# Two weight pieces multiplied side by side at the head of the dense layer and of the recurrent block, and the first two attention pairs' probabilities formed during the projections

## The chip, the cores and the metric

The kernel runs on one core of a Trainium2 chip. The metric is the device time of one execution in microseconds, from the first to the last instruction with what lies around it. The kernel before took 1434.54 us (median of three runs, 1433.47 to 1436.35). The profile is of one further execution of 1437.88 us, of which 1435.7 us are the span of its instructions.

## What is computed

Two layers over 256 tokens of width 1024 in float32. What matters for the change, cut from the reference:

```python
# layer 0
proj = h @ w_in                                   # q, k, v of 16 heads of 64, forget logits
p = softmax(q k^T / 8 + mask (+ F_t - F_s))       # causal; heads 8..15 with a forget bias
o = concat(p @ v) @ w_out
x = x + gate * rms_norm(o)                        # and the next sub-layer's norm and modulation
x = x + gate * rms_norm((silu(h @ w_gate) * (h @ w_up)) @ w_down)     # dense layer, d_ff 2816
# layer 1
proj = h @ w_in                                   # gate branch and u, 1280 each
conv = causal width-4 convolution of u
r, i = sigmoid(conv @ w_a + b_a), sigmoid(conv @ w_x + b_x)           # block diagonal, 10 blocks of 128
hs = linear recurrence; y = gelu(gate branch) * hs; y @ w_out
x = x + gate * rms_norm(...)
x = x + gate * rms_norm(top-2-of-8 expert SwiGLU)                     # d_expert 3584
```

The shifts, scales and gates of all norms come from `silu(c) @ w_ada`.

## The kernel before, in words

All products are made on TensorE (PE) in float32r as three matmuls, high part times high part, high part times low part of the activations, low part of the weights times high part (`mm3`, L404 to L407; a weight's two parts are `whi`, `wlo`, the activations' `hThi`, `hTlo`). One **piece** is 128 output columns of a weight with its 1024 rows: eight blocks of 128 rows, so 24 matmuls of 256 tokens, all into one PSUM bank (`wstat`, L409 to L413).

**The weights** come as one stream of 1 MB pages of two pieces each (class `Stream`). SyncE's queue loads them into six buffers (`raw`). Each piece is split into its two parts: ScalarE (ACT) rounds it to `whi` (L386), VectorE (DVE) subtracts to get `wlo` (L389). Between them the stream holds pieces of `w_ada`, which DVE multiplies and sums with `silu(c)` (L212, 1.2 us each, "ada" below); the tables `ADA_QK`, `ADA_SCORE` and `ADA_OUT` say how many ada pieces are taken at each step. `ws.done` frees a piece and lets later ones be loaded, split or reduced. Each engine runs its instructions in the order in which they were written; engines wait for each other only by semaphores.

**PSUM** has eight banks: four of the tag `B`, handed out in turn by `wbank()`, two of `t`, and `y0` and `y1`. A bank is given again only when the readers of its last use are done. The output projection, the dense layer's down product and the recurrent block's output product are summed in `y0`, `y1` and the two `t` (`y_banks`).

**Attention.** A loop of 16 steps makes the pieces q0, k0, q1, k1 to q7, k7 on PE, each copied out by ACT (L580 or L582); for the first eight DVE and GpSimd (POOL) apply the rotation (`rope`). At step 9 the forget logits are made on PE, and from step 9 on `forget()` spreads their sigmoid, logarithm and running sum, and some small vectors for layer 1, over DVE and ACT: an exponential (L543, L544), a logarithm (L546, L547), each with a load of ACT's function table. Then a second loop goes over p = 0 to 9, where p is a pair of heads: `scores(p)` (eight or sixteen matmuls on PE, then mask and row maximum on DVE, L613 to L617), `exps(p)` (ACT, L626), a reciprocal (DVE, L683) and `norms` (POOL, L634: four diagonal matrices `dg`), and two steps later `turn(p)` (PE, L641 to L643: transposes the probabilities and divides by their sums at once; ACT copies them to `pt`, L644), `heads_out(p)` (PE, L652; ACT copies to `o`, L655), and one step later `out_proj(p)` (PE, L661). So in pass p stand, in this order: scores(p), turn(p-2), exps(p), ada pieces, reciprocal and norms(p), out_proj(p-3), heads_out(p-2), ada pieces.

**Between sub-layers** `finish` applies the norm, PE transposes the result into the four `B` banks (L381), and `make_hT` (L394 to L402) turns it block by block into `hThi` and `hTlo`: ACT scales and shifts (L399), DVE rounds (L388) and subtracts (L389).

**Dense layer.** Six groups of four gate pieces (`fg`), four up pieces (`fu`) and four down pieces (`fd`); gate and up of one piece share a bank, the gate in columns 0 to 255. **Recurrent block.** Pieces `lu` 0 to 9 (the branch u), then `lg` 0 to 9. After each `lu` ACT and DVE run the convolution (L775, L778), ACT and DVE split its result (`ch`, `cl`), and two steps later PE makes the two gates of that block (`gates_mm`, L405 to L407 on `ch`, `cl`), which ACT turns into `rg` and `ig` (L799, L801) and DVE multiplies in (L802). Then come exponential, root and recurrence on ACT and DVE, and the output product `lo`. The experts follow, with most of the bytes.

Of the kernel before, what the change touches and what calls it, by code (L numbers as in the profile page):

```python
# [1 line left out]

# [6 lines left out]
F32 = mybir.dt.float32  # L9
# [121 lines left out]
def trunk_kernel(ctx, tc, xin, cbc, sm_d, at_d, wd, wm, out, stage=9):  # L131
# [282 lines left out]

    def y_banks():
        return [[bank("y0"), bank("y1")], [bank("t", 2), bank("t", 2)]]
# [151 lines left out]

    ADA_QK = [0, 0, 1, 1, 1, 0, 1, 1, 1, 2, 2, 1, 1, 1, 1, 1]
    ADA_SCORE = [2, 0, 1, 1, 2, 2, 3, 1, 3, 1]  # L570
    ADA_OUT = [0, 2, 1, 1, 1, 2, 0, 2, 0, 1]
    pend, fox = None, forget()
    for i in range(16):
        w = ws.next()
        kind, j = w[2]
        b = wbank()
        wstat(b[:, :S], w, hi, lo)
        if j < 4:
            qk32[kind, j] = poolH.tile([P, S], F32, name="qk32", tag="v32", bufs=4)
            A.activation(qk32[kind, j], b[:, :S], AF.Copy)  # L580
        else:
            A.activation(qk[kind, j], b[:, :S], AF.Copy)  # L582
        if i > 8:
            next(fox, None)
        ws.done(ada=ADA_QK[i])
        if pend:
            rope(*pend)
        pend = (kind, j) if j < 4 else None
    pb.close()

    pb = ExitStack()
    poolB = pb.enter_context(tc.tile_pool(name="poolB", bufs=1))
    mask = C("mask")
    pt4 = const.tile([P, 4, 384], F32, name="pt4", tag="hThi", bufs=1)

    def scores(p):
# [5 lines left out]
        sb = [wbank() for _ in range(2)]  # L602
# [42 lines left out]

    def heads_out(p):
        b = wbank()
        for kt in range(2):
            n = 256 - kt * P
            for hh in range(2):  # L650
                c = p * P + hh * 64
                T.matmul(b[hh * 64:hh * 64 + 64, :n], v32[:, kt, c:c + 64],  # L652
                         pt4[:, 2 * (p % 2) + hh, kt * 256:kt * 256 + n], start=kt == 0, stop=kt == 1)
        o = poolB.tile([P, S], F32, name="o", bufs=3)
        A.activation(o, b[:, :S], AF.Copy)  # L655
        return o
# [11 lines left out]
    probs, outs = {}, {}  # L668
    for p in range(10):
# [4 lines left out]
        if p == 7:  # L674
            ws.cap = 3
        if p < 8:
            res, mx = scores(p)
        if 0 <= p - 2 < 8:
# [27 lines left out]
    ws.done(1, ada=1)  # L706
    Y = y_banks()
    for c in range(6):
        n = 4 if c < 5 else 2
        bs = [wbank() for _ in range(n)]  # L710
        acts = []
        for j in range(n):
            w = ws.next("fg")
# [130 lines left out]
    for n in range(2 * N_RNN):  # L844
# [3 lines left out]
        if n < N_RNN:  # L848
            w = ws.next("lu")
            b = wbank()  # L850
            wstat(b[:, :S], w, hi, lo)
# [831 lines left out]
```

## Time and profile before

| | |
|---|---|
| median of three runs | 1434.54 us (1433.47 to 1436.35) |
| profiled execution | 1437.88 us, its span 1435.7 us |
| PE busy | 1380.0 us, 96% of the span |
| DVE busy | 892.1 us, 62% |
| ACT busy | 693.1 us, 48% |
| POOL busy | 44.5 us, 3% |
| bytes read | 474.32 MB, 331 GB/s over the span |
| mean granted TensorE clock | 0.991 of full speed |

A matmul's end in the profile is modelled, and a matmul that waits for an operand after its start was counted can look busy. So on PE the starts of the matmuls are read, and the distance between them, rather than the busy share. In order of time the span holds: attention with its projections to 165 us, the dense layer from 178 to 370 us, the recurrent block from 378 to 485 us, and the experts from there on.

### The profile page before, as it was taken

How to read it: one execution, taken by the hardware profiler on the slowest of the kernel's cores; microseconds unless marked ns; L12 is line 12 of the kernel's file. 1: busy time of each engine (PE TensorE's matmuls, PEld its weight loads, DVE VectorE, ACT ScalarE, POOL GpSimd, SP SyncE). 2: the span in 40 equal slices, each digit the busy share in tenths (PEclk: the TensorE clock that was granted, in tenths of full speed). 3: DMA queues.
4: the chain of work that ended last, by engine and by line, in shares of the span. 5: the costliest groups of instructions: out<-in, count | busy, mean ns of one | idle time of the engine just before them, and what ended most of it. 6: DMA issues, size and time to landing. Idle time of an engine off the chain costs nothing.

```text
span 1435.7 us, 21519 instructions
## 1 busy us (share of the span) xinstructions
PE 1380.0 (96%) x8223; PEld 1008.6 (70%) x8223; DVE 892.1 (62%) x1269; ACT 693.1 (48%) x1022; POOL 44.5 (3%) x62
## 2 busy tenths in 40 slices
PE   5989999999898899999999999999999999999997
PEld 2786589999797678877777767766566566665652
DVE  5787498874798789888666766755333343333321
ACT  2444454443685687976565656743222232321311
POOL 0106200000000000000000000000000000000000
PEclk9999999999999999999999999999999999999999
DMA  9976578886164988699999999999999999998991
GB/s 390 380 269 232 204 284 345 341 314 240 59 219 152 359 319 312 218 364 364 372 398 408 409 390 420 388 370 408 414 398 414 389 365 406 404 410 328 388 374 64
DMA packets 76989, 476.84 MB, mean 332 GB/s; under 512 B 8528, under 2 KB 8528, under 8 KB 28880
## 3 DMA queue, kind: packets, MB, share of 16 engines
q1 hardware_dynamic: 76880, 475.40, 84.8%
q8 instruction: 66, 1.08, 0.3%
q14 instruction: 43, 0.35, 0.1%
HBM read 474.32 MB, written 1.05 MB: 331 GB/s over the span
## 4 chain that ended last, share of the span: by engine, by line
PE 84%; DVE 7%; ACT 4%; DMA 2%; issue 2%; POOL 0%; SPq 0%; ACTq 0%; POOLq 0%; DVEq 0%
PE B L1064 18%; PE B L405 12%; PE B L406 12%; PE B L407 11%; PE y L1064 7%; PE y L407 3%; PE y L406 3%; PE y L405 3%; DVE wlo L389 2%; DMA raw<-in_wm_dram 2%; PE t L1155 1%; PE t L1337 1%; PE y L492 1%; DVE raw L212 1%; PE y L661 1%
## 5 line engine op out<-in xcount | busy, mean ns | idle before, releaser
L389 DVE TENSOR_TENSOR wlo<-raw,whi 128x1024 fp32r<-128x1024 f32 x451 | 541.2, 1221 | 231.5 <-ACT whi L386 196.2
L386 ACT ACTIVATE whi<-raw 128x1024 fp32r<-128x1024 f32 x448 | 465.0, 1057 | 261.4 <-PE B L407 183.9
L1064 PE MATMUL B<-raw,xTc 128*64 128x256 f32 x1792 | 205.3, 382 | 0.0
L405 PE MATMUL B<-hThi,whi 128*128 128x256 f32 x640 | 181.6, 284 | 2.2 <-ACT ge L831 1.7
L406 PE MATMUL B<-hTlo,whi 128*128 128x256 f32 x640 | 180.6, 282 | 0.8
L405 PE MATMUL B<-whi,xTh 128*128 128x512 f32 x448 | 181.3, 405 | 0.0
L407 PE MATMUL B<-hThi,wlo 128*128 128x256 f32 x640 | 178.6, 279 | 0.0
L406 PE MATMUL B<-wlo,xTh 128*128 128x512 f32 x448 | 176.9, 395 | 1.3 <-DVE srt L1384 0.7
L407 PE MATMUL B<-whi,xTl 128*128 128x512 f32 x448 | 176.6, 394 | 0.0
L1064 PEld LDWEIGHTS B<-raw,xTc 128*64 128x64 f32 x1792 | 124.3, 137 | 74.4 <-issue 16.5
L406 PEld LDWEIGHTS B<-hTlo,whi 128*128 128x128 f32 x640 | 120.0, 188 | 4.6 <-DVE hTlo L389 3.6
L405 PEld LDWEIGHTS B<-hThi,whi 128*128 128x128 f32 x640 | 120.2, 188 | 3.8 <-ACT ge L831 1.9
L407 PEld LDWEIGHTS B<-hThi,wlo 128*128 128x128 f32 x640 | 120.0, 187 | 0.0
L212 DVE CUSTOM_DVE_ANT_0 raw<-raw,cond 128x1024 f32<-128x1024 f32 x96 | 113.9, 1217 | 0.0
L405 PEld LDWEIGHTS B<-whi,xTh 128*128 128x128 f32 x448 | 84.1, 188 | 30.4 <-issue 13.2
L1064 PE MATMUL y<-raw,hTc 128*64 128x512 f32 x448 | 101.9, 596 | 0.0
L406 PEld LDWEIGHTS B<-wlo,xTh 128*128 128x128 f32 x448 | 84.2, 188 | 20.7 <-DVE wlo L389 3.6
L407 PEld LDWEIGHTS B<-whi,xTl 128*128 128x128 f32 x448 | 84.1, 188 | 19.5
L1143 DVE TENSOR_TENSOR sg<-sg,B 128x256 f32<-128x256 f32 x35 | 14.6, 418 | 95.6 <-ACT sg L1142 95.6
L1064 PEld LDWEIGHTS y<-raw,hTc 128*64 128x64 f32 x448 | 30.6, 137 | 54.4 <-issue 52.1
L405 PE MATMUL y<-whi,hTh 128*128 128x512 f32 x168 | 67.4, 401 | 0.4 <-ACT hTh L1163 0.4
L407 PE MATMUL y<-whi,hTl 128*128 128x512 f32 x168 | 66.5, 396 | 0.8 <-DVE hTl L1164 0.8
(314 smaller groups left out, 1605.0 us busy)
## 6 DMA issues: line engine op xcount, KB each, us to landing
raw<-in_wm_dram SPq DMA_DIRECT2D x261, 1024.0 KB, 8.8
raw<-in_wd_dram SPq DMA_DIRECT2D x114, 1024.0 KB, 6.4
raw<-in_wm_dram SPq DMA_DIRECT2D x150, 512.0 KB, 8.6
x<-in_x_dram SPq DMA_DIRECT2D x1, 1024.0 KB, 5.2
out_dram<-res SPq DMA_DIRECT2D x4, 256.0 KB, 2.7
sm<-in_sm_dram SPq DMA_DIRECT2D x1, 548.5 KB, 6.8
cond<-in_c_dram SPq DMA_DIRECT2D x1, 512.0 KB, 6.0
at<-in_at_dram SPq DMA_DIRECT2D x1, 320.0 KB, 9.3
```

The source lines that it names most:

```text
L212: V.tensor_tensor_reduce(src, src, cond, 1.0, 0.0, op0=ALU.mult, op1=ALU.add, accum_out=modc[:, col:col + 1])
L386: A.activation(hi, v32, AF.Copy)
L389: V.tensor_tensor(lo, v32, hi.bitcast(F32), op=ALU.subtract)
L405: T.matmul(o, lh, rh, start=start, stop=False)
L406: T.matmul(o, lh, rl, start=False, stop=False)
L407: T.matmul(o, ll, rh, start=False, stop=stop)
L492: T.matmul(vb[h][tt], whole[k][:, t], w[3][:, c], start=k == 0, stop=k == 7)
L661: T.matmul(Y[tt][h], o_of(o)(tt), w[3][:, h * 512:h * 512 + 512], start=p == 0, stop=end)
L1064: T.matmul(o[64 * t:64 * t + 64], xs, w[:, t * n:t * n + n], start=start, stop=stop)
L1143: V.tensor_tensor(g[t], g[t], b[:, 256:], op=ALU.mult)
L1155: T.transpose(b[:, j * P:(j + 1) * P], a[t][:, j * P:(j + 1) * P], ident)
L1337: T.matmul(b, u.pt[t][r, tt * P:(tt + 1) * P], yr[r, j], start=j == 0, stop=j == 1)
```

## The change

Three things are done, all in `trunk_kernel`:

- **Probabilities beside projections.** `scores`, `exps`, `norms` and `turn` are defined before the projection loop. A generator `first_probs(p)` makes scores(p), exps(p) and norms(p) of pairs 0 and 1 in three steps each; from step 10 of the projection loop on one step is taken after each piece. These two scores use the `t` banks. The second loop then starts at p = 2, where turn(0) stands ahead of scores(2). The ada pieces of the first two passes (two and two) are given to pass 2: three behind its exponentials instead of one, three at its end instead of one.
- **Dense layer.** The first two `fg` pieces are multiplied together (`wstat_pair`): for each block of 128 rows the three matmuls of the first piece and then the three of the second, into `y0` and `y1`; the other two of that group use `B`.
- **Recurrent block.** The same for `lu` 0 and `lu` 1.

```diff
+    def wstat_pair(os, ws_, hi, lo):
+
+        for k in range(KT):
+            c = slice(k * P, (k + 1) * P)
+            for o, w in zip(os, ws_):
+                mm3(o, w[0][:, c], w[1][:, c], hi[:, k], lo[:, k], k == 0, k == KT - 1)
...
     def scores(p):
...
-        sb = [wbank() for _ in range(2)]
+        sb = [bank("t", 2) if p < 2 else wbank() for _ in range(2)]
...
+    def first_probs(p):
+
+        res, mx = scores(p)
+        yield
+        sums = exps(res, mx)
+        yield
+        V.reciprocal(sums, sums)
+        probs[p] = res, norms(sums)
+        yield
...
-    ADA_SCORE = [2, 0, 1, 1, 2, 2, 3, 1, 3, 1]
-    ADA_OUT = [0, 2, 1, 1, 1, 2, 0, 2, 0, 1]
-    pend, fox = None, forget()
+    ADA_SCORE = [0, 0, 3, 1, 2, 2, 3, 1, 3, 1]
+    ADA_OUT = [0, 0, 3, 1, 1, 2, 0, 2, 0, 1]
+    pend, fox, head = None, forget(), chain(first_probs(0), first_probs(1))
     for i in range(16):
...
         if i > 8:
             next(fox, None)
+        if i > 9:
+            next(head, None)
         ws.done(ada=ADA_QK[i])
...
-    for p in range(10):
+    for p in range(2, 10):
...
+        if p == 2:
+            turn(0, *probs.pop(0))
         if p < 8:
             res, mx = scores(p)
-        if 0 <= p - 2 < 8:
+        if 1 <= p - 2 < 8:
             turn(p - 2, *probs.pop(p - 2))
...
+    first = [bank("y0"), bank("y1")]
     Y = y_banks()
     for c in range(6):
         n = 4 if c < 5 else 2
-        bs = [wbank() for _ in range(n)]
+        bs = [wbank() for _ in range(n)] if c else first + [wbank() for _ in range(2)]
         acts = []
         for j in range(n):
+            if c == 0 and j < 2:
+                if j:
+                    wstat_pair([b[:, :S] for b in bs[:2]], [ws.next("fg") for _ in range(2)], hi, lo)
+                    for _ in range(2):
+                        ws.done(ada=1)
+                continue
...
         if n < N_RNN:
-            w = ws.next("lu")
-            b = wbank()
-            wstat(b[:, :S], w, hi, lo)
+            if n == 0:
+                two = [bank("y0"), bank("y1")]
+                wstat_pair([b[:, :S] for b in two], [ws.next("lu") for _ in range(2)], hi, lo)
+            if n < 2:
+                b = two[n]
+            else:
+                w = ws.next("lu")
+                b = wbank()
+                wstat(b[:, :S], w, hi, lo)
```

ACT's instructions at the end of the projections, before (q_96 to k_99 are the pieces of steps 12 to 15, `e`, `fza` and `s` belong to `forget()`, `pr` are the probabilities; lines are those of each kernel's own file):

```order
L543 ACT_TABLE_LOAD
L543 ACTIVATE e_720<-e_720 128x10
L544 ACTIVATE fza<-fza 72x256
L546 ACT_TABLE_LOAD
L546 ACTIVATE fza<-fza 72x256
L547 ACTIVATE s_335<-e_721 128x10
L582 ACTIVATE q_96<-B 128x256
L582 ACTIVATE k_97<-B 128x256
L582 ACTIVATE q_98<-B 128x256
L582 ACTIVATE k_99<-B 128x256
L626 ACT_TABLE_LOAD
L626 ACTIVATE pr,sums<-pr,mx 128x128
```

And the same place now, from the third exponential of pair 0 on:

```order
L609 ACTIVATE pr,sums<-pr,mx 128x128
L609 ACTIVATE pr,sums<-pr,mx 128x256
L655 ACTIVATE q_96<-B 128x256
L655 ACTIVATE k_97<-B 128x256
L655 ACTIVATE q_98<-B 128x256
L609 ACTIVATE pr,sums<-pr,mx 128x128
L609 ACTIVATE pr,sums<-pr,mx 128x256
L609 ACTIVATE pr,sums<-pr,mx 128x128
L609 ACTIVATE pr,sums<-pr,mx 128x256
L655 ACTIVATE k_99<-B 128x256
L627 ACTIVATE pt_994<-B 128x384 x2
```

The table load and the exponentials of pair 0 stand right behind `s`, ahead of the copy of q_96; those of pair 1 stand ahead of the copy of k_99.

DVE's instructions at the same place, before (`raw,modc` is an ada piece; `pr,mx` is mask and maximum, and `t` or `B` the bank that it reads):

```order
L554 TENSOR_TENSOR e_722<-e_721,msk 128x10
L212 ISA raw,modc<-raw,cond 128x1024
L212 ISA modc 128x1
L556 RECIPROCAL e_722<-e_722 128x10
L557 TENSOR_TENSOR s_335<-s_335,e_720 128x10
L558 TENSOR_TENSOR s_335<-s_335,e_722 128x10
L559 TENSOR_TENSOR e_720<-e_720,msk 128x10
L560 TENSOR_TENSOR s_335<-s_335,e_720 128x10
L212 ISA raw,modc<-raw,cond 128x1024
```

And now:

```order
L562 TENSOR_TENSOR e_725<-e_724,msk 128x10
L637 RECIPROCAL sums<-sums 128x4
L213 ISA raw,modc<-raw,cond 128x1024
L213 ISA modc 128x1
L564 RECIPROCAL e_725<-e_725 128x10
L565 TENSOR_TENSOR s_335<-s_335,e_723 128x10
L566 TENSOR_TENSOR s_335<-s_335,e_725 128x10
L567 TENSOR_TENSOR e_723<-e_723,msk 128x10
L568 TENSOR_TENSOR s_335<-s_335,e_723 128x10
L596 ISA pr,mx<-t,sm 128x128
L596 ISA mx 128x1
L598 ISA pr,mx<-t,sm 128x256
```

The reciprocal of pair 0's sums and the masks of pair 1 now stand between the ada pieces of the projections (the masks of pair 0 stand earlier, behind `fza`).

PE at the head of the dense layer, before (the transposes, then the first piece):

```order
L381 MATMUL B<-sm,xs 128x128 x16
L405 MATMUL B<-hThi,whi 128x256
L406 MATMUL B<-hTlo,whi 128x256
L407 MATMUL B<-hThi,wlo 128x256
L405 MATMUL B<-hThi,whi 128x256
```

And now (y_1532 and y_1533 are the banks `y0` and `y1`):

```order
L406 MATMUL y_1532<-hThi,whi 128x256
L407 MATMUL y_1532<-hTlo,whi 128x256
L408 MATMUL y_1532<-hThi,wlo 128x256
L406 MATMUL y_1533<-hThi,whi 128x256
L407 MATMUL y_1533<-hTlo,whi 128x256
L408 MATMUL y_1533<-hThi,wlo 128x256
L406 MATMUL y_1532<-hThi,whi 128x256
```

Each block of `hThi` and `hTlo` is now used by six matmuls before the next one is wanted. ACT and DVE keep their order in the dense layer and in the recurrent block.

## Rows read from the trace of the kernel before

**Rows 1.** The chain that ended last: share of the span by engine.

```profile
PE 84%; DVE 7%; ACT 4%; DMA 2%; issue 2%; POOL 0%; SPq 0%; ACTq 0%; POOLq 0%; DVEq 0%
```

**Rows 2.** Stretches: length, busy us of PE, PEld, DVE, ACT, POOL; clock, DMA share, GB/s.

```profile
178.20:184.00 5.80, 5.39 (x26) 3.70 (x27) 5.23 (x16) 4.81 (x8) 0.00 (x0) 1.00 0.00 0
...
456.00:466.00 10.00, 7.25 (x29) 4.94 (x28) 8.08 (x12) 5.07 (x7) 0.00 (x0) 1.00 0.15 42
```

**Rows 3.** PE's timeline, first passes of attention: start, length, line, count, idle before.

```profile
100.52 1.58 PE L611 MATMUL B<-k,q 64*128 64x128 f32 x16
...
108.37 0.79 PE L641 MATMUL B<-dg,pr 128*128 128x128 f32 x2 [4.18 <-DVE mx L617]
...
111.23 2.02 PE L652 MATMUL B<-pt,vall 128*64 128x256 f32 x8
...
116.40 0.46 PE L641 MATMUL B<-dg,pr 128*128 128x128 f32 x2 [1.29 <-ACT o L655]
...
117.14 1.88 PE L661 MATMUL y<-raw,o 128*128 128x512 f32 x4
...
120.67 0.87 PE L652 MATMUL B<-pt,vall 128*64 128x256 f32 x8
...
123.08 0.49 PE L641 MATMUL B<-dg,pr 128*128 128x128 f32 x2
...
124.52 1.02 PE L661 MATMUL y<-raw,o 128*128 128x512 f32 x2
```

**Rows 4.** Stretch of those passes, columns as in rows 2.

```profile
108.40:114.00 5.60, 5.60 (x28) 4.48 (x28) 3.70 (x15) 2.70 (x10) 4.54 (x5) 0.59 0.43 130
```

**Rows 5.** DVE's timeline from the projections into the first pass.

```profile
88.88 1.22 DVE L212 CUSTOM_DVE_ANT_0 raw<-raw,cond 128x1024 f32<-128x1024 f32 x1
...
93.44 0.17 DVE L545 TENSOR_SCALAR e<-e 128x10 f32<-128x10 f32 x1
...
96.11 1.22 DVE L212 CUSTOM_DVE_ANT_0 raw<-raw,cond 128x1024 f32<-128x1024 f32 x1
...
97.89 1.22 DVE L212 CUSTOM_DVE_ANT_0 raw<-raw,cond 128x1024 f32<-128x1024 f32 x1
...
102.02 0.28 DVE L613 CUSTOM_DVE_ANT_0 pr<-B,sm 128x128 f32<-128x128 f32 x1
...
103.33 1.22 DVE L212 CUSTOM_DVE_ANT_0 raw<-raw,cond 128x1024 f32<-128x1024 f32 x1
```

**Rows 6.** ACT's timeline there; the last row is of the chain, of one pair's exponentials.

```profile
91.55 1.28 ACT L546 ACT_TABLE_LOAD   x1
92.85 0.42 ACT L546 ACTIVATE fza<-fza 72x256 f32<-72x256 f32 x1
...
104.87 1.87 ACT pr L626 x8
```

**Rows 7.** POOL's timeline there: the diagonal matrices of pair 1.

```profile
110.54 5.09 POOL L634 TENSOR_SCALAR dg<-sm,sums 128x128 f32<-128x128 f32 x4 [1.06 <-DVE sums L683]
```

**Rows 8.** PE's timeline at the head of the dense layer.

```profile
178.04 0.38 PE L405 MATMUL B<-hThi,whi 128*128 128x256 f32 x1
...
183.66 0.28 PE L407 MATMUL B<-hThi,wlo 128*128 128x256 f32 x1
183.78 0.28 PE L405 MATMUL B<-hThi,whi 128*128 128x256 f32 x1
```

**Rows 9.** Recurrent block: a stretch, what ACT waited for from PE, DVE's and PE's timeline.

```profile
396.00:408.00 12.00, 12.00 (x104) 12.00 (x104) 11.71 (x23) 9.09 (x17) 0.00 (x0) 1.00 0.57 188
...
ACT rg L799 <- PE B L407: 0.5, 1, 0.5
...
406.42 1.51 DVE L778 SCALAR_TENSOR_TENSOR conv<-B,sm,conv 128x255 f32<-128x255 f32 x3
...
417.90 0.28 PE L405 MATMUL B<-ch,whi 128*128 128x256 f32 x1
...
421.44 0.28 PE L405 MATMUL B<-ch,whi 128*128 128x256 f32 x1
```

More of the change, by code (lines that the diff above doesn't have):

```diff
@@ L1 @@
 from contextlib import ExitStack
+from itertools import chain
 import concourse.bass as bass
@@ L566, in forget @@
         yield
-    ADA_QK = [0, 0, 1, 1, 1, 0, 1, 1, 1, 2, 2, 1, 1, 1, 1, 1]
-    ADA_SCORE = [2, 0, 1, 1, 2, 2, 3, 1, 3, 1]
-    ADA_OUT = [0, 2, 1, 1, 1, 2, 0, 2, 0, 1]
-    pend, fox = None, forget()
-    for i in range(16):
-        w = ws.next()
-        kind, j = w[2]
-        b = wbank()
-        wstat(b[:, :S], w, hi, lo)
[L578 to L591, printed above, removed]
     poolB = pb.enter_context(tc.tile_pool(name="poolB", bufs=1))
     mask = C("mask")
-    pt4 = const.tile([P, 4, 384], F32, name="pt4", tag="hThi", bufs=1)
     def scores(p):
@@ L644, in turn @@
             A.activation(pt4[:, 2 * (p % 2) + hh], b[:, :384], AF.Copy)
+    probs = {}
+    def first_probs(p):
[6 more added lines that the diff above has]
+        yield
+    ADA_QK = [0, 0, 1, 1, 1, 0, 1, 1, 1, 2, 2, 1, 1, 1, 1, 1]
+    ADA_SCORE = [0, 0, 3, 1, 2, 2, 3, 1, 3, 1]
+    ADA_OUT = [0, 0, 3, 1, 1, 2, 0, 2, 0, 1]
+    pend, fox, head = None, forget(), chain(first_probs(0), first_probs(1))
+    for i in range(16):
+        w = ws.next()
+        kind, j = w[2]
+        b = wbank()
+        wstat(b[:, :S], w, hi, lo)
+        if j < 4:
+            qk32[kind, j] = poolH.tile([P, S], F32, name="qk32", tag="v32", bufs=4)
+            A.activation(qk32[kind, j], b[:, :S], AF.Copy)
+        else:
+            A.activation(qk[kind, j], b[:, :S], AF.Copy)
+        if i > 8:
+            next(fox, None)
+        if i > 9:
+            next(head, None)
+        ws.done(ada=ADA_QK[i])
+        if pend:
+            rope(*pend)
+        pend = (kind, j) if j < 4 else None
+    pt4 = const.tile([P, 4, 384], F32, name="pt4", tag="hThi", bufs=1)
     def heads_out(p):
@@ L666, in o_of @@
         return lambda tt: t[:, (1 - tt) * P:(2 - tt) * P]
-    probs, outs = {}, {}
-    for p in range(10):
+    outs = {}
+    for p in range(2, 10):
         if p == 3:
@@ L848, in trunk_kernel @@
         if n < N_RNN:
-            w = ws.next("lu")
-            b = wbank()
-            wstat(b[:, :S], w, hi, lo)
+            if n == 0:
[3 more added lines that the diff above has]
+                b = two[n]
+            else:
+                w = ws.next("lu")
+                b = wbank()
+                wstat(b[:, :S], w, hi, lo)
         else:
```

## The prediction

> **What bounds the kernel now.** I read the chain of waits first: PE carries 84% of it, DVE 7%, ACT 4%, DMA 2% [rows 1]. So time is won where PE stands still, and nowhere else. The second view is of stretches, for what a gain in an early stage is worth at the end. At the head of the dense layer the DMA engines are idle, share 0.00, and before the last output products share 0.15 [rows 2]: the six buffers are full, and the next load waits for a buffer to come free, not for bandwidth. The weight stream is thus paced by the engines up to the experts and moves with them: a gain at any of the three places should arrive at the end whole. The third view is PE's timeline at the three places.
>
> In attention PE ends the projections and does the scores of pairs 0 and 1 from 100.52; then it waits 4.18 us, until 108.37, for pair 0's probabilities, and 1.29 us before 116.40 [rows 3]. In between its clock is down: 0.59 granted in 108.40 to 114.00 [rows 4], so turn(0) takes 111.23 - 108.37 = 2.86 us where the turn at 123.08 takes 1.44. The first output product starts at 117.14, the second at 124.52 [rows 3]; from there the passes follow each other without a wait of PE. At the head of the dense layer the first piece takes 183.78 - 178.04 = 5.74 us, though its matmuls follow each other at 183.78 - 183.66 = 0.12, 2.88 for 24 [rows 8]: it waits for each block of hThi and hTlo. The recurrent block begins in the same way.
>
> **Attention, step by step.** In steps 10 to 15 PE does the same pieces plus two scores of 1.58 / 2 = 0.79 [rows 3], so it ends at 102.1 instead of 100.52. Up to the second output product it then has three turns of 1.44, two scores of 0.79, a heads_out of 0.87, a heads_out and the longer scores of pair 4 together 2.41 (123.08 - 120.67), and one output product of 3.53 (120.67 - 117.14) [rows 3]: 12.7, so 114.8 against 124.52. That is 9.7 us, the most that this part can give. The new order does not let PE run through, because the work given to DVE and ACT comes in the stretch in which DVE is never idle: from 88.88 it goes without a gap to the masks at 102.02 [rows 5].
>
> I follow the chain with rows. Masks of one pair cost 103.33 - 102.02 = 1.31. Masks of pair 0 go in at 88.88 (their scores are ready by then), so the small operation that ACT's logarithm waits for moves from 93.44 to 94.75 [rows 5]. Behind that logarithm (I allow 0.4) come a table load of 1.28 and the exponentials of 1.87 [rows 6]: done at 98.3. DVE reaches the reciprocal at 96.11 + 1.31 = 97.42 and stands still for about 0.9; then an ada piece and small ones (97.89 - 96.11 = 1.78), masks of pair 1 from 100.2 to 101.5, the rest up to the old masks (102.02 - 97.89 = 4.13) and a reciprocal: masks of pair 2 from 105.7 to 107.0. The scores of pair 2 wait for a bank that the copy of the last piece frees, and that copy stands behind pair 1's exponentials (101.5 + 1.87 and a copy and a handoff of 0.6 together, 104.0): they are done at 104.8, and it is DVE that is late. On ACT the copy of `o` of pair 0 stands behind pair 2's exponentials: 107.0 + 1.87 + 0.6 = 109.5. The second half of turn(1) needs that bank, so the first output product starts at 109.5 + 0.72 = 110.2, against 117.14, and ends at 113.7.
>
> Next comes what the tables moved. Behind masks 2 DVE has six ada pieces (1.14 each, from 96.11 and the like) and a reciprocal before masks 3: 107.0 + 6.9 + 0.4 = 114.3. heads_out(1) takes over a bank that the first half of masks 3 frees, at 114.9, where PE is free at 113.7. Then 2.41 and 1.44 give the second output product at **118.75, 5.8 us earlier**. POOL's diagonals may last 5.09 beside ada pieces [rows 7]; for pair 1 that is 104.7 + 5.3 = 110.0, half a us behind what I took for turn(1), and still ahead of the wait at 114.9. In the passes behind, DVE catches up, since it has fewer ada pieces there than PE has time for. Ends for this part: 9.7 if DVE does not bind, and 3 if every handoff is late by another 0.5. I take 5.8.
>
> One rule speaks against the part. The rows show a table load of 1.28 whose next operation starts 0.02 after it, 92.85 behind 91.55 [rows 6]. The Trainium skill (ScalarE: Activation LUTs, What ACT_TABLE_LOAD costs) states about 1.28 us for the load and about 1.38 more to drain; the trace shows no drain. By the page the chain through pair 0's exponentials would be 1.4 longer and this part worth 4.4.
>
> **Dense layer.** Now each block is used six times, 6 x 0.12 = 0.72, and the blocks come every 5.74 / 8 = 0.72: a second piece fits into the waits. Behind the last block's third matmul of the first piece, at 183.66, only the second piece's three are left: 183.66 + 4 x 0.12 = 184.14 for the third piece, against 183.78 + 2.88 = 186.66 [rows 8]. That is 2.5 us; I take **2.4**, for a short lag behind the last block. The third and fourth pieces are wanted 2.5 us earlier, but three were split before the layer and the fourth is the first that DVE splits behind hTlo, so it is in time. `y0` is wanted by the down product only behind the up pieces. The dense layer is paced by PE behind this (DVE catches up in each group), so the gain is kept. Ends: 2.0 and 2.6.
>
> **Recurrent block.** The same arithmetic gives PE 2.4 us, but here PE is not alone. From 396 to 408 DVE is busy for 11.71 of 12.00 us, and ACT waits for PE only once for 0.5 from 386 to 418 [rows 9]: convolution, split and gate of each block run as a loop of ACT and DVE that PE does not pace. PE gets ahead until it must wait for a bank that the convolution two blocks back has read. The convolution of block 6 ends at 406.42 + 1.51 = 407.93 in any case. From there to the last gates PE has four pieces and three pairs of gate products; a piece and a pair take 421.44 - 417.90 = 3.54, a pair 6 x 0.12: 407.93 + 4 x 3.54 - 0.72 = 421.37, against 421.44 [rows 9]. **0.1 us** is left, since the chain to the end goes on from these gates through ACT. Ends: 0 and 2.4.
>
> **The sum.** 5.8 + 2.4 + 0.1 = 8.3 us: span 1435.7 to 1427.4, the profiled execution's time 1437.88 to about 1429.6. That execution lies 3.3 above the median of the runs, 1434.54; I set the difference against the median: **1426.2 us**.
>
> **The rivals.**
> - DVE's backlog does not bind: attention gives 9.7, the rest 2.5, 1422.3. For it: the backlog is a sum of many small terms. Against it: DVE has no gap from 88.88 on [rows 5]. 0.08.
> - ACT and DVE follow PE in the recurrent block: 2.4 instead of 0.1, 1423.9. For it: a share of DVE of 0.98 leaves a little. Against it: that DVE is fed by ACT, not by PE [rows 9]. 0.12.
> - The chain between ACT and DVE in the projections costs more (later copies, slow diagonals): attention gives 2 to 3, 1429.5. 0.14.
> - The change doesn't do what it says: the probabilities are no earlier, since pair 2 is the new late one, and only the dense layer gains: within 0.2%, 1431.7 to 1434.5. Against it: turn(0) and turn(1) no longer wait for masks that follow the projections. 0.05.
> - Slower: the clock. PE now has four short waits between 103 and 115 instead of one long. If its clock falls to 1.2 GHz there and stays down, each us of PE work costs another us (2.86 against 1.44 for a turn [rows 3]). It decides at 8.3 us of work at half clock; from 107 to the end of pass 5 that is 8.8 + 7.4 (124.52 - 117.14): 1442.4. The Trainium skill (TensorE: Matmul & The Clock Gate, What's actually happening) has the low clock as the default that activity lifts, which would be this rival's cause. Against it: the 1.29 us wait before 116.40 is followed by a turn at full speed, 117.14 - 116.40 for half of it [rows 3]. 0.03.
>
> **How the numbers follow.** The forecast has 0.58. The range goes from 1422.5 to 1430.5: it holds the forecast with its own ends (attention 4.5 to 7, dense 2.0 to 2.6, 1425 to 1428), the recurrent block's rival and most of the late chain. About 0.2% can be told from no change in a measurement of this kernel, 2.9 us. Faster by more than that: 0.58 + 0.08 + 0.12 + 0.14 = 0.92; within: 0.05; slower: 0.03.
>
> **What would show it.** Right: turn(0) directly behind the last piece; first output product 7 us earlier, second 5 to 6; heads_out(1) waiting for masks on DVE; the clock near 1.00 throughout; third dense piece 6.1 us behind the first block; last gates of the recurrent block as far behind its first block as before. Wrong: a granted clock under 0.8 in the first passes; PE waiting in the projections for banks that ACT frees late; DVE idle before masks 2; the experts taking longer by what the front gained.

## The result and the profile after

The changed kernel takes 1427.88 us (median of 6 runs, 1427.07 to 1430.61), the kernel before 1436.06 (6 runs, 1433.47 to 1436.91): ratio 0.9950, 95% interval 0.9941 to 0.9960, which is 5.7 to 8.5 us less, 7.2 in the middle; the medians lie 8.2 apart. The forecast was 8.3 us less. It was set against a median of 1434.54 from three runs; with more runs the kernel before stood at 1436.06, 1436.32, 1435.66 and 1435.47, so most of the distance from the forecast's 1426.2 to 1427.88 is that base.

The profiled executions are 1437.88 (span 1435.7) and 1427.77 us (span 1425.6), 10.1 us apart. Not all of that is the change, and the first thing to read is what of it is not. These are stretches at the very start, in which both programs are the same; the columns are length, busy us of PE, PEld, DVE, ACT, POOL, then the granted clock, DMA share and GB/s. Before:

```profile
20.00:25.00 5.00, 5.00 (x8) 1.94 (x8) 4.95 (x10) 0.02 (x1) 0.00 (x0) 0.58 1.02 423
```

After:

```profile
20.00:25.00 5.00, 5.00 (x10) 2.07 (x9) 4.96 (x11) 0.00 (x0) 0.00 (x0) 1.00 1.01 421
```

In the one execution PE was at 1.2 GHz over most of that stretch, in the other at 2.4. At the first rotation product, ahead of everything that the change touches, the second is 0.92 us ahead (53.72 against 54.64). From here on I count every stage from that product, in each kernel's own trace.

PE's timeline of the changed kernel through the first passes of attention (start, length, line, count, idle time before with what ended it) answers to [rows 3]:

```profile
101.61 0.38 PE L624 MATMUL B<-dg,pr 128*128 128x128 f32 x2
...
105.69 0.92 PE L594 MATMUL B<-k,q 64*128 64x128 f32 x6 [0.35 <-DVE mx L598]
...
109.20 0.49 PE L624 MATMUL B<-dg,pr 128*128 128x128 f32 x2 [1.72 <-POOL dg L617]
...
109.97 1.88 PE L681 MATMUL y<-raw,o 128*128 128x512 f32 x4
...
113.50 0.87 PE L672 MATMUL B<-pt,vall 128*64 128x256 f32 x8
...
117.59 0.46 PE L624 MATMUL B<-dg,pr 128*128 128x128 f32 x2 [0.69 <-ACT o L675]
...
118.34 1.88 PE L681 MATMUL y<-raw,o 128*128 128x512 f32 x4
```

The wait of 4.18 us is gone: the first turn follows the last piece of the projections. Three small waits are left, 0.35, 1.72 and 0.69. The first output product starts at 109.97, which is 117.14 - 109.97 - 0.92 = 6.25 us earlier; the second at 118.34, 124.52 - 118.34 - 0.92 = 5.26 earlier. What ends these waits is on DVE, ACT and POOL. First DVE (reciprocals, and the first masks of pairs 1, 2 and 3):

```profile
97.45 0.18 DVE L637 RECIPROCAL sums<-sums 128x4 f32<-128x4 f32 x1 [0.88 <-ACT pr L609]
...
99.50 0.28 DVE L596 CUSTOM_DVE_ANT_0 pr<-t,sm 128x128 f32<-128x128 f32 x1
...
103.78 0.17 DVE L637 RECIPROCAL sums<-sums 128x4 f32<-128x4 f32 x1
...
105.00 0.28 DVE L596 CUSTOM_DVE_ANT_0 pr<-B,sm 128x128 f32<-128x128 f32 x1
...
113.77 0.28 DVE L596 CUSTOM_DVE_ANT_0 pr<-B,sm 128x128 f32<-128x128 f32 x1
```

Then ACT (a table load, the exponentials of pairs 0, 2 and 3, the copy of `o` that stands behind the last):

```profile
94.26 1.28 ACT L609 ACT_TABLE_LOAD   x1
95.55 0.40 ACT L609 ACTIVATE pr<-pr,mx 128x128 f32<-128x128 f32 x1
...
106.58 0.40 ACT L609 ACTIVATE pr<-pr,mx 128x128 f32<-128x128 f32 x1 [2.68 <-DVE mx L600]
...
115.32 0.40 ACT L609 ACTIVATE pr<-pr,mx 128x128 f32<-128x128 f32 x1 [4.66 <-DVE mx L600]
...
117.09 0.36 ACT L675 ACTIVATE o<-B 128x256 f32<-128x256 f32 x1
```

And POOL, pair 1's four diagonals:

```profile
104.05 5.09 POOL L617 TENSOR_SCALAR dg<-sm,sums 128x128 f32<-128x128 f32 x4 [3.10 <-DVE sums L637]
```

At the head of the dense layer the transposes, the first block and the third piece of the changed kernel are these rows, for 178.04 in [rows 8]:

```profile
168.38 1.07 PE L382 MATMUL B<-sm,xs 128*128 128x128 f32 x8 [2.36 <-DVE xs L367]
...
171.58 0.58 PE L406 MATMUL y<-hThi,whi 128*128 128x256 f32 x1
...
179.51 0.28 PE L406 MATMUL B<-hThi,whi 128*128 128x256 f32 x1
```

179.51 - 171.58 = 7.93 us. In the kernel before, the third piece starts at 186.61:

```profile
186.61 0.28 PE L405 MATMUL B<-hThi,whi 128*128 128x256 f32 x1
```

That is 8.57 behind the first block, so 0.64 us are won there where 2.4 were forecast. The stretches of the changed kernel say why; the first answers to [rows 4], the other two lie over the pair:

```profile
108.40:114.00 5.60, 4.80 (x20) 2.47 (x22) 5.57 (x16) 1.17 (x4) 4.50 (x3) 1.00 0.87 331
171.60:176.20 4.60, 4.60 (x22) 4.43 (x21) 4.25 (x13) 3.39 (x8) 0.00 (x0) 0.51 0.00 0
176.20:179.60 3.40, 3.40 (x31) 3.40 (x30) 3.19 (x7) 3.40 (x5) 0.00 (x0) 1.00 0.16 19
```

In attention the clock is 1.00 in place of 0.59. Over the first part of the dense pair it is 0.51, that is 1.2 GHz: 22 matmuls in 4.60 us, then 31 in 3.40.

At the end of the recurrent block the last piece but one of the gate branch (`lg` 8, "last gates" below) waits 1.68 us for ACT, as before. Near the block's start PE now waits at two places where it did not:

```profile
380.97 0.38 PE L406 MATMUL B<-ch,whi 128*128 128x256 f32 x1 [0.74 <-ACT ch L387]
...
386.09 0.38 PE L406 MATMUL B<-hThi,whi 128*128 128x256 f32 x1 [0.27 <-ACT ig L830]
...
433.31 0.39 PE L406 MATMUL B<-hThi,whi 128*128 128x256 f32 x1 [1.68 <-ACT ge L860]
```

From the block's first product (370.97) to the last gates are 62.34 us. Before it was 440.96 - 378.20 = 62.76, so 0.42 are won. DVE's convolution of block 6, counted in the same way, is no earlier: 399.32 - 370.97 = 28.35, and 406.42 - 378.20 = 28.22 before [rows 9].

```profile
399.32 1.51 DVE L807 SCALAR_TENSOR_TENSOR conv<-B,sm,conv 128x255 f32<-128x255 f32 x3
```

Behind that comes a second piece that is not the change's: from the router's selection product to the end the spans of all the profiled kernels of this study are 936.2 to 938.2 us, in no order with their edits. The two compared here are 938.2 (before) and 936.4 (after). So of the 10.1 us between the two spans 0.92 lie ahead of the change and 1.8 in the experts, and the rest is 7.4; the medians say 8.2.

### The profile page after: what moved, and what is told of

It is laid out like the page before. It is cut to its first block, busy times and chain, and to the rows that moved or that the text cites. A ratio compares the mean times of both kernels' runs of the same rounds, so it can differ in the third digit from the quotient of the medians.

```text
span 1425.6 us, 21512 instructions
## 1 busy us (share of the span) xinstructions
PE 1376.5 (97%) x8223; PEld 1008.6 (71%) x8223; DVE 892.1 (63%) x1269; ACT 691.9 (49%) x1022; POOL 47.8 (3%) x62
## 4 chain that ended last, share of the span: by engine, by line
PE 55%; DVE 1%; DMA 1%; issue 0%; ACT 0%; ACTq 0%
PE B L1099 19%; PE y L1099 7%; PE B L406 7%; PE B L408 6%; PE B L407 6%; PE y L406 2%; PE y L408 2%; PE y L407 2%; PE t L1190 1%; PE t L1372 1%; DVE wlo L390 1%; DMA raw<-in_wm_dram 1%; PE t L1077 0%; PE t L1078 0%; PE B L1482 0%
## 5 line engine op out<-in xcount | busy, mean ns | idle before, releaser
L406 PE MATMUL B<-hThi,whi 128*128 128x256 f32 x592 | 167.7, 283 | 2.0 <-ACT ge L860 1.7
L407 PE MATMUL B<-hTlo,whi 128*128 128x256 f32 x592 | 165.5, 280 | 0.0
L408 PE MATMUL B<-hThi,wlo 128*128 128x256 f32 x592 | 165.3, 279 | 0.0
L406 PEld LDWEIGHTS B<-hThi,whi 128*128 128x128 f32 x592 | 111.2, 188 | 3.7 <-ACT ge L860 1.9
L407 PEld LDWEIGHTS B<-hTlo,whi 128*128 128x128 f32 x592 | 111.1, 188 | 0.7 <-issue 0.2
L408 PEld LDWEIGHTS B<-hThi,wlo 128*128 128x128 f32 x592 | 110.9, 187 | 0.0
L407 PE MATMUL y<-wlo,hTh 128*128 128x512 f32 x168 | 66.4, 395 | 0.0
```

The costliest lines, as they stand in the source:

```text
L406: T.matmul(o, lh, rh, start=start, stop=False)
L407: T.matmul(o, lh, rl, start=False, stop=False)
L408: T.matmul(o, ll, rh, start=False, stop=stop)
```

## The experiments

Stages of each profiled execution in us, counted as said above: first and second output product from the first rotation product; the dense layer's third piece, and its first down product, from the layer's first block; the last gates of the recurrent block (`lg` 8) from its first product. Then the time, the median of the runs, and the ratio to the kernel before with its interval.

| kernel | out 1 | out 2 | third piece | down | last gates | us | ratio |
|---|---|---|---|---|---|---|---|
| before | 62.50 | 69.88 | 8.57 | 25.52 | 62.76 | 1436.06 | |
| changed | 56.25 | 64.62 | 7.93 | 24.89 | 62.34 | 1427.88 | 0.9950 (0.9941 to 0.9960) |
| attention alone | 56.26 | 64.64 | 8.56 | 25.52 | 62.77 | 1429.79 | 0.9955 (0.9941 to 0.9968) |
| dense alone | 62.50 | 69.88 | 6.27 | 23.23 | 62.76 | 1433.34 | 0.9981 (0.9972 to 0.9990) |
| recurrent alone | 62.50 | 69.89 | 8.56 | 25.52 | 62.37 | 1436.50 | 0.9997 (0.9988 to 1.0006) |
| longer filler | 56.25 | 64.63 | 6.28 | 23.24 | 62.36 | 1427.48 | 0.9936 (0.9923 to 0.9950) |
| changed again | 56.24 | 64.62 | 6.52 | 23.48 | 62.34 | 1428.16 | 0.9948 (0.9935 to 0.9962) |
| steps swapped | 55.84 | 64.37 | 6.87 | 23.82 | 62.35 | 1427.56 | 0.9941 (0.9927 to 0.9954) |
| swapped, filler | 55.32 | 63.69 | 6.24 | 22.56 | 62.76 | 1426.57 | 0.9937 (0.9923 to 0.9950) |
| two diagonals on ACT | 55.72 | 64.47 | 6.27 | 23.23 | 62.35 | 1426.94 | 0.9940 (0.9928 to 0.9953) |
| pieces later | 55.88 | 63.26 | 6.27 | 23.23 | 62.35 | 1428.42 | 0.9949 (0.9935 to 0.9964) |
| all | 54.78 | 62.16 | 6.27 | 23.23 | 62.54 | 1425.81 | 0.9934 (0.9919 to 0.9949) |

### Each part alone

**Attention.** The two pairs of the dense layer and the recurrent block are undone in the changed kernel:

```
-    first = [bank("y0"), bank("y1")]
-        bs = [wbank() for _ in range(n)] if c else first + [wbank() for _ in range(2)]
+        bs = [wbank() for _ in range(n)]
-            if c == 0 and j < 2:
-                if j:
-                    wstat_pair(...)
```

> Only the attention part of the change is kept; dense layer and recurrent block stand as before. Theory (the attention part carries most of the gain): 5.5 us less than the kernel before, the first output product about 6.2 us earlier, and no stretch at half clock between 106 and 113 us. Rival (the three parts share the gain as forecast, with 2.4 us in the dense layer): the attention part alone gives 5.8 of the 8.2, so the two agree here to 0.5 us and what tells them apart is the next kernel. Rival (nothing but a shift of the clock's low stretches, which differ from execution to execution): less than 2 us.

Measured: 0.9955, that is 4.6 to 8.5 us less. Both output products come as early as in the changed kernel, and the same two waits stand in the trace, 1.73 for the diagonals and 0.70 for the copy of `o`. So the attention part carries most of the gain and has nothing to do with the pairs, and the rival of less than 2 us falls. One thing stays in it: in all three executions with the old attention the clock was low over part of these passes (0.59 in [rows 4]), so no run shows what the old order would take there at 1.00. The clock is low over the head of the dense layer here too:

```profile
171.50:176.00 4.50, 4.50 (x20) 4.27 (x19) 4.14 (x13) 3.34 (x7) 0.00 (x0) 0.52 0.00 0
```

Yet the single pieces lose nothing by it: 25.52 to the down products, as before. They wait for each block of hThi and hTlo anyway, and half the clock fits into these waits.

**Dense layer.** The pair of `fg` pieces is put into the kernel before, and nothing else:

```
+    first = [bank("y0"), bank("y1")]
+        bs = [wbank() for _ in range(n)] if c else first + [wbank() for _ in range(2)]
+            if c == 0 and j < 2:
+                if j:
+                    wstat_pair([b[:, :S] for b in bs[:2]], [ws.next("fg") for _ in range(2)], hi, lo)
```

> Only the pair of the dense layer is kept; all else stands as before. In the changed kernel the third piece began 7.93 us behind the first block (8.56 before, 6.1 forecast). Theory (the granted clock of 0.50 over the first half of the pair took the gain): where the clock is back at 1.00 before the first block, the third piece begins 6.1 us behind it and the kernel takes 2 to 2.4 us less; where it is low over half the pair, 7.9 us and 0.6 us less. Rival (the pair waits for its operands, whatever the clock): 7.9 us at full clock too, with waits on ACT or DVE between its blocks.

PE's timeline at its first block and third piece:

```profile
177.87 0.49 PE L405 MATMUL y<-hThi,whi 128*128 128x256 f32 x1
...
184.14 0.28 PE L405 MATMUL B<-hThi,whi 128*128 128x256 f32 x1
```

The stretch over them:

```profile
177.80:184.20 6.40, 6.40 (x51) 6.12 (x50) 5.80 (x17) 5.20 (x9) 0.00 (x0) 0.97 0.00 0
```

At a clock of 0.97 the third piece starts 184.14 - 177.87 = 6.27 us behind the first block, and the down products 2.29 us earlier; the time is 2.7 us less (1.4 to 4.0). There the pair is worth what was forecast, at a clock of 2.4 GHz over nearly all of it, and the rival of operands that come late whatever the clock falls.

**Recurrent block.** The pair of `lu` pieces alone is put into the kernel before:

```
+            if n == 0:
+                two = [bank("y0"), bank("y1")]
+                wstat_pair([b[:, :S] for b in two], [ws.next("lu") for _ in range(2)], hi, lo)
```

> Only the pair of the recurrent block is kept. Theory (ACT and DVE pace the block, PE waits later for what it saved): the third piece starts 2.3 us earlier behind the first block than before, the last gate piece 0 to 0.4 us earlier, and the time moves by 0 to 0.4 us. Rival (PE paces): 2.3 us less.

The block's first product and its last gates on PE's timeline:

```profile
376.26 0.39 PE L405 MATMUL y<-hThi,whi 128*128 128x256 f32 x1 [0.39 <-DVE hThi L388]
...
438.63 0.39 PE L405 MATMUL B<-hThi,whi 128*128 128x256 f32 x1 [1.68 <-ACT ge L838]
```

438.63 - 376.26 = 62.37, 0.39 less than before, and a time that cannot be told from no change (0.9997). The third piece came 6.28 us behind the first block, 2.3 earlier, and the last gates got a sixth of that. As in the changed kernel PE gives the rest back near the block's start, where it waits for ACT (0.74 us for `ch`, 0.28 for `ig`); the rival of 2.3 us falls.

### The clock over the dense pair

**Longer filler.** In the changed kernel two more filler products stand in PE's idle time of 2.36 us ahead of the transposes:

```
         warm(banks[3], *(bridge or (last[-1][0][0], WARM[0])))
+        if bridge:
+            warm(banks[3], v32[:, 0], 2)
```

> The changed kernel, with two more filler products (four instructions, 1.8 us) on PE in its idle 2.36 us ahead of the dense layer's transposes; they read the tile of values, so that no weight's buffer is held longer. Theory (the clock took the dense pair's gain): the clock stays at 1.00 from 160 to 180 us, the transposes' second half takes 1.1 us in place of 2.0, the third piece begins 6.1 us behind the first block, and the time is 1.5 to 2.5 us below the changed kernel's. Rival (the clock falls there whatever PE does, or the fillers are too few): third piece 7.9 us behind, time as the changed kernel's. Rival (the expert stage waits for its weights anyway and swallows what the dense layer gives): third piece 6.1 us behind, time as the changed kernel's.

PE's timeline:

```profile
165.38 1.88 PE L434 MATMUL B<-vall 128*128 128x512 f32 x4
167.90 1.06 PE L382 MATMUL B<-sm,xs 128*128 128x128 f32 x8 [0.64 <-DVE xs L367]
169.42 1.09 PE L382 MATMUL B<-sm,xs 128*128 128x128 f32 x8 [0.46 <-DVE xs L367]
170.84 0.38 PE L406 MATMUL y<-hThi,whi 128*128 128x256 f32 x1 [0.33 <-DVE hThi L389]
...
177.12 0.28 PE L406 MATMUL B<-hThi,whi 128*128 128x256 f32 x1
```

The stretches over it:

```profile
165.40:170.80 5.40, 4.02 (x21) 2.26 (x19) 3.33 (x9) 2.35 (x6) 1.10 (x2) 1.00 0.55 196
170.80:177.20 6.40, 6.28 (x49) 6.08 (x50) 5.82 (x16) 5.19 (x9) 0.00 (x0) 1.00 0.00 0
```

The clock stays at 1.00, the third piece is 6.28 us behind, and the second half of the transposes takes 1.09. In the stage that is 1.65 us better than the changed kernel's profiled execution. In the time it can't be told: the medians are 1427.48 against 1427.88, the ratios 0.9936 against 0.9950 (2.0 us) with intervals that overlap, where 1.5 to 2.5 less were expected. The rival with the experts has no support: from the router on this execution takes 936.7 us, the changed kernel's 936.4. The next run says more.

**The changed kernel again**, with no edit:

> The changed kernel once more, beside the two that follow, for a second look at where its clock is low. Theory (the low stretch over the dense pair is what this program gives, since PE stands idle for 2.36 us at the same place each time): low again from about 6.9 us behind the first filler ahead of the dense layer for 6.8 us, third piece 7.9 us behind the first block. Rival (where the low stretches fall is up to the execution): the pair at full clock in this one, third piece 6.2 to 6.4 us behind. Time 1427.9 +- 0.7.

First block and third piece on PE's timeline:

```profile
171.87 0.58 PE L406 MATMUL y<-hThi,whi 128*128 128x256 f32 x1
...
178.39 0.28 PE L406 MATMUL B<-hThi,whi 128*128 128x256 f32 x1
```

The stretches over them:

```profile
171.80:173.00 1.20, 1.20 (x6) 0.96 (x5) 1.08 (x5) 0.71 (x2) 0.00 (x0) 0.50 0.00 0
173.00:178.40 5.40, 5.40 (x47) 5.40 (x47) 4.92 (x13) 4.69 (x8) 0.00 (x0) 0.97 0.00 0
```

It is the same program with the same idle time of 2.36 us ahead of it, and here the low clock ended soon after 173: 6.52 us, 2.05 less than before. So the 7.93 of the first execution was that execution, not the program, and the first theory falls. Of the 1.65 us by which the kernel with the longer filler beats the first execution, the changed kernel itself gives 1.41 in another one.

The delay goes with the time that the low clock covers of the pair: about 4.6 us in the first execution, 1.4 here and 2.2 in the kernel with the steps swapped below, where the third piece comes 1.66, 0.25 and 0.60 us later than the 6.27 of a pair at full clock. What the longer filler does is open, but not without a sign: in the three executions with it the clock is 1.00 over the transposes and the pair, and without it, with the change's attention, it is low over a part of them in five of six.

### What is left in attention

**Steps swapped.** In each of the last projection passes the step of the first two pairs goes ahead of the forget gates' step:

```
+        if i > 9:
+            next(head, None)
         if i > 8:
             next(fox, None)
-        if i > 9:
-            next(head, None)
```

> The changed kernel with two lines swapped: in each of the last projection passes the step of the first two attention pairs now stands ahead of the step of the forget gates, on ACT and DVE. Theory (what is left of PE's waits in the attention comes from DVE's queue: the reciprocal of pair 0 stands 0.88 us behind ACT, and masks and reciprocal of pair 1 behind it, so that POOL's diagonals of pair 1 end 1.72 us late for PE): reciprocal of pair 0 at 95 in place of 97.45 with no wait, PE's wait of 1.72 us for the diagonals falls under 0.4, the first output product 1.3 to 1.7 us earlier; the second only 0.9 earlier, the stall that DVE no longer has, since the masks of pair 3 stand behind six weight pieces there; time 0.9 us less than the changed kernel. Rival (ACT paces: the exponentials of pair 1 now need the table loaded again, 1.28 us): the diagonals of pair 1 as late as before and the time the same.

The first output product came 0.41 us earlier, and the wait for the diagonals stayed at 1.72. This execution had a low clock just there, which a row shows:

```profile
108.00:112.00 4.00, 3.28 (x9) 2.25 (x10) 4.00 (x10) 1.09 (x3) 2.90 (x2) 0.61 0.79 285
```

The rival falls for the diagonals: they start 0.93 earlier, though a table load now stands ahead of pair 1's exponentials. The time is 0.6 below that of the changed kernel run beside it (1428.16), less than can be told apart.

**Swapped, with the longer filler**, and the recurrent block's pair undone (`two`, as above):

> The swap of the kernel above and the longer filler ahead of the dense layer together, and the recurrent block's pair undone, which alone moved nothing. Theory (the parts add): third piece of the dense layer 6.3 us behind the first block, gates of the recurrent block as far behind its first block as before, and 1.5 to 2.5 us less than the changed kernel: 1425.4 to 1426.4. Rival (what is won ahead of the expert stage is given back there, where PE waits for weights from memory): within 0.7 us of the changed kernel.

Here the clock is 1.00 there, and the swap can be read: DVE's reciprocal of pair 0, POOL's diagonals of pair 1, PE's wait for them.

```profile
94.67 0.17 DVE L639 RECIPROCAL sums<-sums 128x4 f32<-128x4 f32 x1
...
102.75 5.09 POOL L619 TENSOR_SCALAR dg<-sm,sums 128x128 f32<-128x128 f32 x4 [3.59 <-DVE sums L639]
...
107.90 0.49 PE L626 MATMUL B<-dg,pr 128*128 128x128 f32 x2 [1.72 <-POOL dg L619]
```

DVE's stall of 0.88 at pair 0's reciprocal is gone, and both output products are 0.93 us earlier. The wait of 1.72 is unchanged, so half of the expectation falls: everything moved up together, since the second half of the turn needs POOL's third and fourth diagonal, and POOL takes 5.09 for four. In time it is 1426.57 (1425.74 to 1427.38) beside 1428.16 (1427.24 to 1429.59) for the changed kernel on the same chip: 1.6 less, as expected in size, though the intervals of the two ratios overlap. Not all of it need be the edits: the down products start 0.67 us earlier than in the other kernels with the pair at full clock (22.56 against 23.23), since the matmuls ahead of them stand 0.113 us apart in place of 0.118, at the same granted clock of 1.00; no row says why.

**Two diagonals on ACT.** Of pair 1's four, ACT makes the last two:

```
-            G.tensor_scalar(dg[:, j], ident, sums[:, j:j + 1], None, op0=ALU.mult)
+            if second and j > 1:
+                A.activation(dg[:, j], ident, AF.Copy, scale=sums[:, j:j + 1])
+            else:
+                G.tensor_scalar(dg[:, j], ident, sums[:, j:j + 1], None, op0=ALU.mult)
```

> The changed kernel with the last two of pair 1's four diagonals made on ACT, which stands idle there from 103.9 to 106.6 us, in place of POOL. In all looks so far PE's wait of 1.72 us ahead of the second half of the second turn stood, also where the reciprocal ahead came 0.9 us earlier, since POOL takes 5.09 us for four. Theory (POOL's pace sets the first output product, DVE's backlog the second): the wait of 1.72 falls under 0.3 and the first output product comes 1.4 to 1.7 us earlier, the second at most 0.3 earlier, since masks of pair 3 stand behind six weight pieces; time as the changed kernel's. Rival (one chain, whoever is late first): both products 1.4 us earlier, and the time as much less.

ACT's two diagonals, POOL's two, and PE's two new waits:

```profile
103.45 0.69 ACT L618 ACTIVATE dg<-sm,sums 128x128 f32<-128x128 f32 x2 [0.85 <-DVE sums L640]
...
103.51 2.06 POOL L620 TENSOR_SCALAR dg<-sm,sums 128x128 f32<-128x128 f32 x2 [3.10 <-DVE sums L640]
...
104.57 1.25 PE L675 MATMUL B<-pt,vall 128*64 128x256 f32 x8 [0.99 <-ACT pt L630]
...
108.13 0.49 PE L627 MATMUL B<-dg,pr 128*128 128x128 f32 x2 [0.59 <-ACT o L678]
```

The wait for POOL is gone, but the first product comes only 0.53 us earlier, not 1.4: the copies of the probabilities stand behind the diagonals on ACT, and then the bank that the copy of `o` frees is the late one. That copy is the very chain on which the forecast built the first product. The second product is 0.15 earlier, as expected. The time of 1426.94 is one that this cannot explain; its ratio's interval overlaps the changed kernel's.

**Pieces later.** Four of the six weight pieces between the masks of pairs 2 and 3 go one pass back:

```
-    ADA_SCORE = [0, 0, 3, 1, 2, 2, 3, 1, 3, 1]
-    ADA_OUT = [0, 0, 3, 1, 1, 2, 0, 2, 0, 1]
+    ADA_SCORE = [0, 0, 1, 3, 2, 2, 3, 1, 3, 1]
+    ADA_OUT = [0, 0, 1, 3, 1, 2, 0, 2, 0, 1]
-        if p == 3:
+        if p == 4:
             gate_cols(0, 2, 1)
```

> The changed kernel with four of the six weight pieces, that DVE reduces between the masks of pair 2 and those of pair 3, put one pass later (two before the masks of pair 3, six behind them in place of two). Theory (DVE's backlog holds the second output product through masks, exponentials and the copy of pair 1's output): masks of pair 3 some 4.6 us earlier, PE's wait of 0.69 us ahead of the second half of the third turn gone, the second output product 0.7 us earlier, and the time 0.7 us less. Rival (the four pieces hold the next pair's masks): a new wait of PE in the pass behind, third output product as late as before, time the same.

POOL's diagonals of pair 1, PE's one wait of over 0.4 us left in the first passes, and DVE's masks of pair 3:

```profile
103.95 4.03 POOL L617 TENSOR_SCALAR dg<-sm,sums 128x128 f32<-128x128 f32 x4 [3.10 <-DVE sums L637]
...
108.75 0.46 PE L624 MATMUL B<-dg,pr 128*128 128x128 f32 x2 [1.38 <-ACT o L675]
...
109.66 0.28 DVE L596 CUSTOM_DVE_ANT_0 pr<-B,sm 128x128 f32<-128x128 f32 x1
```

The masks of pair 3 come 4.0 us earlier, the wait of 0.69 is gone, and the second output product is 1.36 earlier, twice what was expected: the first came 0.37 earlier too, and the third turn takes 1.44 in place of 118.34 - 115.97 = 2.37. DVE's backlog did hold it. The rival falls: PE has no new wait in the pass behind, and the third output product is 1.36 earlier too (72.62 us behind the first rotation product, 73.98 in the changed kernel). The time (1428.42, runs from 1425.00 to 1430.29) does not show it: its runs lie further apart than the 1.4 us in question.

**All of it**, with both edits above, the swap, the filler and the single recurrent pieces:

> All of it: the two kernels above, the swap of the two steps, the longer filler, and the recurrent block's pair undone. Theory (the waits follow each other on PE, and the parts add): first output product 2.4 us earlier than in the changed kernel, second 2 to 2.4, third piece of the dense layer 6.3 us behind the first block, 1423.5 to 1425.5. Rival (the next wait in line, or the expert stage, takes it): as the swap with the longer filler, 1426.6.

The first product is 1.47 us earlier (2.4 expected; the wait of 0.59 for `o` is left), the second 2.46, the third piece 6.27. With 1425.81 us (1424.04 to 1429.77) it has the lowest median here, just above the 1423.5 to 1425.5 expected; its ratio's interval overlaps the changed kernel's, so a gain over it is suggested, not settled.

## Why the prediction was right, point by point

**What bounds.** PE's standing still was the thing to remove, and the experts gave nothing back: their length varies by 2 us from execution to execution in no order with the edits. The chain of waits of the changed kernel, for [rows 1], says less than before; it can be followed back only 57% of the span:

```profile
PE 55%; DVE 1%; DMA 1%; issue 0%; ACT 0%; ACTq 0%
```

**Attention: 5.8 forecast, 5.26 in the trace.** The mechanism held but for two steps. With the offset of 0.92 added, masks of pair 2 start at 105.92 (105.7 forecast), masks of pair 3 at 114.69 (114.3), and DVE's stall at pair 0's reciprocal is 0.88 (0.9). The two steps that were off:

- The first output product was put at 110.2 from the copy of `o`, while the sum of the same paragraph had POOL's diagonals done at 110.0 and passed them over, as half a us behind the turn and ahead of a later wait. They were done at 109.14 + 0.92 = 110.06, and the second half of the turn waited for them: 110.89. A sum was made along one of two chains that end 0.5 us apart, and the later one decides.
- The wait for masks 3 was put at heads_out(1). heads_out(1) did not wait; the same lateness came one step on, in the second half of the third turn, through the exponentials of pair 3 (ACT idle 4.66 for the masks) and the copy of `o` at 117.09. The cause was right, as the pieces put later show, and the place was wrong.

**The table load.** The row has the load at 94.26 for 1.28 and its exponential at 95.55, so nothing drains in between. The Trainium skill (ScalarE: Activation LUTs, What ACT_TABLE_LOAD costs) states about 1.38 us more for a drain. The trace does not agree: between the load's end and its exponential lie 0.01 us, and attention was worth 5.26, not the 4.4 that would follow.

**Dense layer: 2.4 forecast.** This is the term that was mis-sized for the execution profiled: 0.63 us at the down products in the first execution, 2.04 in the second, 2.28 or 2.29 where the clock was up (2.96 in one kernel, by the closer matmuls told of above). The arithmetic of six uses of a block in 0.72 us was right at 2.4 GHz; the step that failed is that it took 0.12 us a matmul from a stretch with the clock at 1.00 [rows 2, 8] and never asked whether the pair would run in such a stretch. At 1.2 GHz six matmuls take 6 x 0.21 (4.60 / 22) = 1.26, more than the blocks' 0.72, and the waits that were to be filled no longer exist. Single pieces lose nothing at the low clock (25.52 with it and without), so no stage of the kernel before could show the price.

**Recurrent block: 0.1 forecast, 0.39 to 0.42 measured** in all seven profiled executions with that pair. The reason was right in kind, since the convolutions keep their times and PE gives back what it saved. The place was wrong: PE was to wait for a bank behind block 6, and it waits for ACT at the first gates, 0.74 and 0.27 us. From there to the last gates it runs without a wait, so the 0.4 left is not the 0.1 of the forecast's sum. The rival with 2.4 us falls.

**The clock.** The forecast had it near 1.00 in attention, and a rival in which it falls there. In eight of the nine profiled executions with the change's attention it is 1.00 there; in one (steps swapped) it was 0.61 from 108 to 112, and that cost 0.93 - 0.25 = 0.7 us at the second output product, by the kernel with the same swap and the clock up, not the rival's price, since PE came back to 2.4 GHz while it worked. The Trainium skill (TensorE: Matmul & The Clock Gate, What's actually happening) has the low clock as the default that activity lifts. The rows agree in kind: it fell behind a standstill of PE and rose while PE was busy. Whether it falls at all behind a given standstill no row ahead of it tells: behind the same 2.36 us it was low from 169.3 to 176.1 in the changed kernel's first execution, until shortly after 173 in its second, and in the kernel with the pieces later it stayed up.

**The sum.** 5.26 + 0.63 + 0.42 = 6.3 us are the three terms in the profiled execution, and about 1.1 more lie elsewhere: 0.28 ahead of the dense layer and 0.65 behind the last gates, where the two executions had their low clock at other times, and 0.13 between. With the dense pair at its worth at 2.4 GHz the three would be 8.0. So it is in part luck that the medians' 8.2 meets the forecast's 8.3 so closely: an attention term 0.5 us too high and a dense one up to 1.8 too high met a recurrent one 0.3 too low and what the low clock gave elsewhere, and the middle of the ratio says 7.2. By their ratios the parts alone are worth 6.5, 2.7 and 0.4; that sums to 9.6, which their intervals allow.

What stays open is how often the low clock covers the dense pair, and so what the pair is worth on average; whether the longer filler keeps the clock up; and whether the kernel with all edits is really 2 us below the changed one.

## What to carry to other kernels

Filling an engine's waits with more of its own work pays only at the pace at which that work runs there: take the matmul's duration at the lower clock too, and see whether the waits are still there. Where two chains end within half a us of each other, carry both to the end of the sum, since the later one sets the time and its owner (here POOL) is the next to relieve. An early stage can be read to 0.1 us from a trace if it is counted from a common instruction ahead of the change, while the time of the whole kernel scatters by 1 to 2 us.

## What had not been expected of the hardware

- The same program has its low clock at other places in other executions. Two executions of the changed kernel gave 7.93 and 6.52 us for the same 48 matmuls, and the very start differs by 0.92 us between two executions in code that no edit touched.
- POOL's four diagonal matrices take 5.09 us with four weight pieces of DVE beside them, 4.03 with two, and 2.35 with none (pair 0 in the kernel before). That DVE slows POOL fits, and was not tried by itself.
